# Down projection by seven block products over groups of feature tiles, in a hybrid decoder layer on one core

## The chip, the cores and the metric

The kernel runs on one core of a Trainium2 chip. The metric is the device time of one execution in microseconds (us); less is better.

## The reference

The layer normalises x (2048 tokens of width 1024, float32), runs two token mixers side by side, adds their output projection to the residual, and then does the part that this case is about:

```
hn = rms_norm(h, ffn_norm_w)
gate, up = split(hn @ w_gate_up)            # 1024 -> 2 x 2816
h = h + (silu(gate) * up) @ w_down          # 2816 -> 1024
return rms_norm(h, final_norm_w)
```

## The kernel before

The tokens are worked on in two halves of 1024; a half is two chunks (c) of 512 tokens, or eight tiles (g) of 128. The mixers of both halves come first, then for each half the up projection (`ffn_up`) and the down projection (`ffn_down`). One core has TensorE (PE), VectorE (DVE), ScalarE (ACT), GpSimd (POOL) and SyncE (SP), which issues all DMAs in order.

Every product of two float32 matrices is made of three matmuls: each operand is split into a high part, cast on ACT (L198), and the rest, a subtraction on DVE (L199). The high parts are multiplied with each other, and each with the other's rest. `split` is the helper; its source and its cast are both in SBUF.

The up projection already uses 2x2 blocks with seven products (p1 to p7) for a pair j of feature tiles (2 x 128 of the 2816 features, 11 pairs). Its results, four 128x512 tiles a11, a12, a21, a22 (feature tile, chunk), are written to DRAM by `store`. Element sums go through `tt_` (L484), on DVE or on GpSimd. The down projection takes the 22 feature tiles one by one for each chunk: it loads the activation tile (`ad`) and a 128x1024 weight tile (`raw_d`), splits both, and adds into eight PSUM banks (`pd`, L697 to L699), all of PSUM. After the last tile the banks are added to the residual `hd`, normalised (`rstd_of`: squares on ACT, a power on GpSimd) and scaled (L717).

`norm_h` belongs to the end of the mixers: for a token tile g it normalises h (`rstd_of`, squares `jk_hs` at L190; scaling at L816), transposes it on TensorE (`tp_hs`, L213), and ACT copies it out of PSUM (`hths`, L819). Five of these, for the second half, are left over and are called between the first seven products of the up projection of the first half. The framework orders the instructions of each engine by its own model; the written order is only a start.

Of the kernel before, what the change touches and what calls it, by code (L numbers as in the profile page):

```python
# [8 lines left out]
F32 = mybir.dt.float32  # L9
# [4 lines left out]
P = 128  # L14
# [8 lines left out]
T = 1024  # L23
# [12 lines left out]
def hybrid_layer(ctx: ExitStack, tc: tile.TileContext, x, x_t, norm_w, cols, w_in, gate_w, w_out, w_gu, w_down, out):  # L36
# [452 lines left out]

    def acts(src, nm):  # L490
        ops = {}
# [7 lines left out]
        def load(k):  # L499
            if k == 0:  # L500
                for name in ("p1", "p5", "p6", "p7", "p2"):
                    ops[name] = [block(f"act_{LET[name]}{s}_{nm}") for s in range(2)]
            b11, b12 = (xin(f"{t}{k}_{nm}") for t in ("b11_", "b12_"))
            b21, b22 = (page(f"{t}{k}_{nm}") for t in ("b21_", "b22_"))
# [10 lines left out]
        def two(k):  # L515
            b11, b12, b21, b22 = pages[k]
            tt_(b11, b22, b11, SUB_)
            tt_(b12, b22, b12, SUB_, nc.gpsimd)
            put("p2", k, b21)
            put("p6", k, b11)  # L520
            tt_(b21, b21, b11, SUB_)
            put("p7", k, b12)
            held.append((b22, b21))

# [10 lines left out]
        return ops, steps, [lambda: rest(0), lambda: rest(1)]  # L535

# [62 lines left out]
    def ffn_up(half, bops, between=()):  # L599
        between = list(between)  # L600
        q0 = half * 2 * NPAIR
        for q in range(q0, q0 + 2 * NPAIR):
# [7 lines left out]
            for i, name in enumerate(ORDER):  # L610
# [12 lines left out]
                elif name == "p7":  # L623
# [3 lines left out]
                    if m == 0:  # L627
                        nc.scalar.activation(out=e5, in_=e5, func=AF.Silu)
                        sg22 = e5
                    else:  # L630
                        tt_(e5, e5, sg22, MUL, nc.gpsimd)
                        store(half, j, 1, 1, e5)
                elif name == "p2":
                    if m == 0:
                        sg11 = page("sg11" + nm)
                        nc.scalar.activation(out=sg11, in_=b1, func=AF.Silu)
                    else:
                        tt_(sg11, sg11, b1, MUL)
                        store(half, j, 0, 0, sg11)
                elif name == "p3":  # L640
                    tt_(e1, u2, b3, ADD)
                    if m == 0:
                        nc.scalar.activation(out=e1, in_=e1, func=AF.Silu)
                        sg12 = e1
                    else:
                        tt_(e1, e1, sg12, MUL)
                        store(half, j, 0, 1, e1)
                else:
# [4 lines left out]
                    else:  # L653
                        tt_(u2, u2, sg21, MUL)
                        store(half, j, 1, 0, u2)
                if nxt is not None and not end:
# [7 lines left out]

    def store(half, j, u, c, p):
        nc.sync.dma_start(out=a_d[half][2 * j + u][c], in_=p)


    def ffn_down(half, c, extra=()):
        extra = list(extra)  # L670
# [3 lines left out]
        def ready(f):  # L674
            if f >= NF or f in ops:
                return
            nm = f"d{half}_{c}_{f}"
            p = xin("a" + nm)
# [6 lines left out]
            split((hi, lo), raw)  # L685
            ops[f] = (a, hi, lo)

        ready(0)
        for f in range(NF):
            ready(f + 1)  # L690
            ready(f + 2)
            a, whi, wlo = ops.pop(f)
            for tt in range(TPC):
                tsl = slice(tt * P, (tt + 1) * P)
                for n in range(2):
                    ps, nsl = banks[tt][n], slice(n * CW, (n + 1) * CW)
                    nc.tensor.matmul(ps, lhsT=a[:, 0, tsl], rhs=whi[:, nsl], start=(f == 0), stop=False)  # L697
                    nc.tensor.matmul(ps, lhsT=a[:, 0, tsl], rhs=wlo[:, nsl], start=False, stop=False)  # L698
                    nc.tensor.matmul(ps, lhsT=a[:, 1, tsl], rhs=whi[:, nsl], start=False, stop=(f == NF - 1))  # L699
            if f >= 6 and extra:  # L700
                extra.pop(0)()
        for e in extra:
            e()
        wfin = wvec(2, f"wfin{half}_{c}")
        for tt in range(TPC):
            g = c * TPC + tt
            r0 = half * T + g * P
            hp = []
            for n in range(2):
                p = page(f"hd{half}_{g}_{n}")  # L710
                nc.sync.dma_start(out=p, in_=h_d[half][g][n])
                tt_(p, p, banks[tt][n], ADD)
                hp.append(p)
            rs = rstd_of(hp, f"f{half}_{g}")
            for n in range(2):
                nsl = slice(n * CW, (n + 1) * CW)
                v.scalar_tensor_tensor(out=hp[n], in0=hp[n], scalar=rs, in1=wfin[:, nsl], op0=MUL, op1=MUL)  # L717
                nc.sync.dma_start(out=out[r0 : r0 + P, nsl], in_=hp[n])
# [3 lines left out]
    a_d = [[[dram.tile([P, CW], F32, name=f"a{i}_{k}_{c}") for c in range(2)] for k in range(NF)] for i in range(2)]  # L722

    bops = {}
    for half in range(2):
# [80 lines left out]
        else:  # L806
            bops[0], st, last = acts(hn_d[0], "0")
# [15 lines left out]

        later = []
        for c in range(NC):
            todo = len(steps[c])
            for n in range(2):
                wo = ws.take(4)
                for tt in range(TPC):
# [8 lines left out]
                    if n == 1:  # L838
                        later.append(lambda half=half, g=g, wffn=wffn, hp=hp: norm_h(half, g, wffn, hp))
                    while len(later) > 1 and (n, c) != (1, 1):  # L840
                        later.pop(0)()
                    i = n * TPC + tt + 1
                    while steps[c] and todo - len(steps[c]) < -(-todo * i // 8):
                        steps[c].pop(0)()
                    if half == 1 and c == 1 and n == 1 and tt == 0:
                        sums_start(0)
                        sums(0).make(0)
                        sums(0).done.add(0)
        if half == 0:
            xt = [b["xn"] for b in boxes]  # L850
# [11 lines left out]
    for half in range(2):  # L862
        ffn_up(half, bops[half], later if half == 0 else ())
        for c in range(NC):
            extra = ()
            if half == 0 and c == 1:
                bops[1], steps, last = acts(hn_d[1], "1")
                extra = steps + last
            ffn_down(half, c, extra)
        if half == 0:  # L870
            q = 2 * NPAIR
            sums_start(q)
# [3 lines left out]
            sums(q + 1).load(0)  # L876
            sums(q + 1).load(1)


# [66 lines left out]
```

## Time and profile before

| what | value |
|---|---|
| median of three runs | 2232.57 us (2226.35 to 2233.69) |
| profiled execution | 2235.64 us, of which its span is 2233.8 us |
| mean granted TensorE clock | 0.988 |
| TensorE busy | 2166.1 us, 97% of the span |
| down projection of the two halves | 1320 to 1559 us and 1984 to 2223 us of the span |

The span is what the profiler sees of the program; the 1.8 us beside it lie around it. A busy TensorE says that some matmul was under way, not how fast they follow each other.

### The profile page before, as it was taken

Reading aid. Unit: us, or ns where it says so; the run is one execution under the profiler, and the core shown is the slowest. Engines: PE = TensorE matmul, PEld = TensorE weight load, DVE = VectorE, ACT = ScalarE, POOL = GpSimd, SP = SyncE. Lnnn points to the kernel's source line nnn. Section 1 sums busy time; section 2 is a strip of 40 time slices with the busy share of each in tenths; the row PEclk is TensorE's granted clock in tenths of the full one; section 3 lists DMA queues with packets and bytes.
Section 4 is the critical chain, followed back from the end, with each engine's and each line's share of the span. In section 5 each row is a group of like instructions: output and inputs, shape, how many; then the busy total and the mean of one; then the engine's idle time right before and its main releaser. Section 6 shows DMA issues by size and latency. Waiting matters only on the chain.

```text
span 2233.8 us, 27050 instructions
## 1 busy us (share of the span) xinstructions
PE 2166.1 (97%) x10184; PEld 1787.4 (80%) x10184; DVE 1273.9 (57%) x2097; ACT 974.1 (44%) x1603; POOL 250.3 (11%) x229
## 2 busy tenths in 40 slices
PE   8999999999999999799999999999999999999998
PEld 6777788787777887688888888888788888888886
DVE  5577655635677458566565643584756565543534
ACT  5477754445667544433333332353333333322322
POOL 1111111101111001111111100010211011100000
PEclk9999999999999999899999999999999999999999
DMA  6111105741011166322222255573422222255552
GB/s 217 57 38 39 38 19 193 263 157 38 29 38 30 37 185 211 119 89 94 76 95 76 87 188 148 161 236 119 128 85 94 76 95 76 95 195 149 184 151 95
DMA packets 122899, 251.36 MB, mean 113 GB/s; under 512 B 11152, under 2 KB 27536, under 8 KB 122768
## 3 DMA queue, kind: packets, MB, share of 16 engines
q1 hardware_dynamic: 122768, 249.63, 35.3%
q8 instruction: 80, 1.31, 0.2%
q14 instruction: 51, 0.42, 0.1%
HBM read 201.35 MB, written 48.23 MB: 112 GB/s over the span
## 4 chain that ended last, share of the span: by engine, by line
PE 78%; ACT 9%; DVE 6%; DMA 3%; issue 1%; POOL 1%; SPq 0%; DVEq 0%; POOLq 0%; ACTq 0%
PE quad_g L579 11%; PE quad_e L579 11%; PE quad_a L579 11%; PE pd L699 7%; PE pd L698 7%; PE pd L697 7%; PE quad_f L579 5%; PE pb L226 1%; PE pb L227 1%; PE pb L225 1%; PE pa L225 1%; DMA raw_o<-in_w_out 1%; PE pa L226 1%; PE poh L238 1%; PE pa L227 1%
## 5 line engine op out<-in xcount | busy, mean ns | idle before, releaser
L698 PE MATMUL pd<-wlo_d,ad 128*128 128x512 f32 x704 | 273.9, 389 | 0.0
L697 PE MATMUL pd<-whi_d,ad 128*128 128x512 f32 x704 | 273.5, 389 | 0.0
L699 PE MATMUL pd<-whi_d,ad 128*128 128x512 f32 x704 | 273.2, 389 | 0.0
L199 DVE TENSOR_TENSOR ad<-ad,ad 128x512 fp32r<-128x512 f32 x88 | 62.4, 710 | 224.1 <-ACT ad L198 217.4
L198 ACT CAST ad<-ad 128x512 fp32r<-128x512 f32 x88 | 54.8, 623 | 289.2 <-PE pd L698 277.9
L484 POOL TENSOR_TENSOR e<-u,e 128x512 f32<-128x512 f32 x44 | 78.0, 1772 | 707.3 <-DVE u L484 367.8
L698 PEld LDWEIGHTS pd<-wlo_d,ad 128*128 128x128 f32 x704 | 132.1, 188 | 27.5
L697 PEld LDWEIGHTS pd<-whi_d,ad 128*128 128x128 f32 x704 | 132.2, 188 | 27.4
L699 PEld LDWEIGHTS pd<-whi_d,ad 128*128 128x128 f32 x704 | 132.2, 188 | 27.4
L579 PE MATMUL quad_f<-act_f,wgu_f 128*128 128x512 f32 x528 | 129.8, 395 | 4.8 <-DVE h L836 3.3
L579 PE MATMUL quad_e<-act_e,wgu_e 128*128 128x512 f32 x528 | 129.1, 393 | 2.8 <-ACT wgu_e L198 1.9
L579 PE MATMUL quad_a<-act_a,wgu_a 128*128 128x512 f32 x528 | 128.2, 392 | 0.0
L579 PE MATMUL quad_g<-act_g,wgu_g 128*128 128x512 f32 x528 | 127.4, 390 | 0.0
L579 PE MATMUL quad_g<-act_d,wgu_d 128*128 128x512 f32 x528 | 127.1, 389 | 0.0
L579 PE MATMUL quad_a<-act_b,wgu_b 128*128 128x512 f32 x528 | 127.0, 389 | 0.0
L579 PE MATMUL quad_e<-act_c,wgu_c 128*128 128x512 f32 x528 | 126.8, 389 | 0.0
L199 DVE TENSOR_TENSOR wlo_d<-raw_d,whi_d 128x1024 fp32r<-128x1024 f32 x88 | 110.0, 1250 | 22.6 <-ACT whi_d L198 18.4
L579 PEld LDWEIGHTS quad_f<-act_f,wgu_f 128*128 128x128 f32 x528 | 100.7, 191 | 26.5 <-ACT act_d L198 3.7
L579 PEld LDWEIGHTS quad_e<-act_e,wgu_e 128*128 128x128 f32 x528 | 100.0, 190 | 24.7 <-ACT wgu_e L198 2.4
L484 DVE TENSOR_TENSOR u<-u,quad_g 128x512 f32<-128x512 f32 x88 | 60.5, 687 | 100.0 <-PE quad_g L579 100.0
L579 PEld LDWEIGHTS quad_a<-act_a,wgu_a 128*128 128x128 f32 x528 | 99.9, 189 | 20.8
L579 PEld LDWEIGHTS quad_g<-act_g,wgu_g 128*128 128x128 f32 x528 | 99.5, 189 | 20.8
(260 smaller groups left out, 4698.5 us busy)
## 6 DMA issues: line engine op xcount, KB each, us to landing
raw<-in_w_gu SPq DMA_DIRECT2D x88, 512.0 KB, 4.1
raw_d<-in_w_down SPq DMA_DIRECT2D x88, 512.0 KB, 3.6
raw_in<-in_w_in SPq DMA_DIRECT2D x48, 512.0 KB, 3.6
ad<-a SPq DMA_DIRECT2D x88, 256.0 KB, 2.6
raw_o<-in_w_out SPq DMA_DIRECT2D x32, 512.0 KB, 4.5
a<-e SPq DMA_DIRECT2D x44, 256.0 KB, 4.2
x<-in_x SPq DMA_DIRECT2D x32, 256.0 KB, 5.4
xrh<-in_x SPq DMA_DIRECT2D x32, 256.0 KB, 4.0
```

The lines of the kernel that those rows point to most:

```text
L198: nc.scalar.copy(out=dst[0], in_=src)
L199: v.tensor_tensor(out=dst[1], in0=src, in1=f(dst[0]), op=ALU.subtract)
L225: nc.tensor.matmul(ps, lhsT=whi[:, ks], rhs=hi, start=(k == 0), stop=False)
L226: nc.tensor.matmul(ps, lhsT=wlo[:, ks], rhs=hi, start=False, stop=False)
L227: nc.tensor.matmul(ps, lhsT=whi[:, ks], rhs=lo, start=False, stop=(k == KT - 1))
L238: nc.tensor.matmul(ps, lhsT=hi, rhs=wlo[:, ks], start=False, stop=False)
L484: (e or v).tensor_tensor(out=out, in0=a, in1=b, op=op)
L579: nc.tensor.matmul(ps, lhsT=w[:, s, ks], rhs=x, start=first and k + n == 0, stop=k == 3 and n == 2, skip_group_check=not first)
L697: nc.tensor.matmul(ps, lhsT=a[:, 0, tsl], rhs=whi[:, nsl], start=(f == 0), stop=False)
L698: nc.tensor.matmul(ps, lhsT=a[:, 0, tsl], rhs=wlo[:, nsl], start=False, stop=False)
L699: nc.tensor.matmul(ps, lhsT=a[:, 1, tsl], rhs=whi[:, nsl], start=False, stop=(f == NF - 1))
```

## The change

The down projection becomes a 2x2 block product as well: feature tiles of a pair (u) and the two chunks on one side, feature tiles and the two column halves of the weights on the other. Seven products do the work of eight. A product runs over a group of four pairs (eight feature tiles), 48 matmuls of 128x512: four token tiles (tt), four pairs (q), three matmuls each. The first half has two such groups; its last three pairs are done as before (`down_plain`, 6 feature tiles). The second half has groups of four, four and three pairs.

The sums of activations are made on GpSimd in `store`, and seven tiles instead of four are written to DRAM. The sums of weights are made in place, on GpSimd (two of them in `make`, for p6, one for p1) and on DVE (`wdt`). The results are added to the residual in SBUF, which is now loaded before the first product: ACT copies p1 (`e1`) and p5 (`e5`) out of PSUM, DVE adds a bank to SBUF for five products, and GpSimd makes four additions per token tile. `norm_h` is cut into `scale_h` and `turn_h`, and a turn is called two places later than its scaling. In `acts` (operands of the second half's up projection) all seven pairs of blocks are now made at once. The diff, cut:

```diff
-    def store(half, j, u, c, p):
-        nc.sync.dma_start(out=a_d[half][2 * j + u][c], in_=p)
...
+    def store(half, j, a11, a12, a21, a22):
+        if (half, j) in PLAIN:
+            for u, c, p in ((0, 0, a11), (1, 0, a12), (0, 1, a21), (1, 1, a22)):
+                nc.sync.dma_start(out=a_d[half][2 * j + u][c], in_=p)
+            return
+        s1, s2, s3, s4 = (xin(f"as{i}_{half}_{j}") for i in range(4))
+        g = nc.gpsimd
+        tt_(s1, a21, a22, ADD, g)
+        tt_(s2, s1, a11, SUB_, g)
+        tt_(s3, a11, a21, SUB_, g)
+        tt_(s4, a12, s2, SUB_, g)
+        for name, p in (("p1", a11), ("p2", a12), ("p4", a22), ("p5", s1), ("p6", s2), ("p7", s3), ("p3", s4)):
+            nc.sync.dma_start(out=ao_d[half][name][j], in_=p)
...
+    DORDER = ("p1", "p2", "p6", "p5", "p3", "p7", "p4")
...
+        def make(self, i, q):
+            name = DORDER[i]
...
+            b = {k: t[:, q, :] for k, t in self.b.items()}
+            if name == "p6":
+                if q == 0:
+                    self.t2 = block(f"wdt_{self.nm}", F32)
+                tt_(self.t2[:, q, :], b[1, 1], b[0, 0], SUB_)
+            x = {"p1": b[0, 0], "p2": b[1, 0], "p5": b[0, 0], "p3": b[1, 1], "p7": b[0, 1], "p4": b[1, 0]}.get(name)
+            if name == "p6":
+                x = self.t2[:, q, :]
+            split([self.w[name][s][:, q, :] for s in range(2)], x)
+            split([self.a[name][q // 2][s][:, q % 2, :] for s in range(2)], self.raws[i][q // 2][:, q % 2, :])
+            if name == "p1":
+                tt_(b[0, 0], b[0, 1], b[0, 0], SUB_, nc.gpsimd)
+            elif name == "p6":
+                tt_(b[1, 0], b[1, 0], self.t2[:, q, :], SUB_, nc.gpsimd)
+                tt_(b[0, 1], b[1, 1], b[0, 1], SUB_, nc.gpsimd)
...
+        groups[0].load()
+        fetch(0)
+        for q in range(4):
+            make(0, q)
+        fetch(1)
+        for s, (gr, i) in enumerate(seq):
...
+            if name in ("p1", "p5"):
+                ma = [bank(f"pda{name[1]}_{tt}_{nm}") for tt in range(TPC)]
+            elif name in ("p6", "p7"):
+                mb = [aux(f"pdb{name[1]}_{tt}_{nm}") for tt in range(TPC)]
+            ps_ = mb if name in ("p6", "p7", "p4") else ma
+            a, w = gr.a.pop(name), gr.w.pop(name)
+            first = name in ("p1", "p6", "p5", "p7")
+            for tt in range(TPC):
...
+                for q in range(gr.n):
+                    ahi, alo = (a[q // 2][z][:, q % 2, tsl] for z in range(2))
+                    whi, wlo = (w[z][:, q, :] for z in range(2))
+                    for n, (x, y) in enumerate(((ahi, whi), (ahi, wlo), (alo, whi))):
+                        nc.tensor.matmul(
+                            ps, lhsT=x, rhs=y, start=first and q + n == 0, stop=q == gr.n - 1 and n == 2, skip_group_check=not first
+                        )
+                h00, h01 = hp[tt]
+                h10, h11 = hp[TPC + tt]
+                if name == "p1":
+                    e1[tt] = late(f"e1_{tt}_{nm}")
+                    nc.scalar.copy(out=e1[tt], in_=ps)
+                elif name == "p2":
+                    tt_(h00, h00, ps, ADD)
+                elif name == "p6":
+                    tt_(e1[tt], e1[tt], ps, ADD)
+                    tt_(h01, h01, e1[tt], ADD, nc.gpsimd)
+                elif name == "p5":
+                    e5[tt] = xin(f"e5_{tt}_{nm}")
+                    nc.scalar.copy(out=e5[tt], in_=ps)
+                    tt_(h10, h10, e1[tt], ADD, nc.gpsimd)
+                elif name == "p3":
+                    tt_(h01, h01, ps, ADD)
+                    tt_(h11, h11, e1[tt], ADD, nc.gpsimd)
+                    if end and last:
+                        finish(half, tt, hp[tt])
+                elif name == "p7":
+                    tt_(e5[tt], e5[tt], ps, ADD)
+                    tt_(h11, h11, e5[tt], ADD, nc.gpsimd)
+                else:
+                    tt_(h10, h10, ps, ADD)
+                    if end and last:
+                        finish(half, TPC + tt, hp[TPC + tt])
+                make(s + 1, tt)
...
+            if name == "p5" and not end:
+                groups[groups.index(gr) + 1].load()
...
-        def norm_h(half, g, wffn, hp):
-            nm = f"hs{half}_{g}"
-            rs = rstd_of(hp[g], nm)
+        def scale_h(half, g, wffn, hp):
+            rs = rstd_of(hp[g], f"hs{half}_{g}")
             for n in range(2):
                 p = hp[g][n]
                 v.scalar_tensor_tensor(out=p, in0=p, scalar=rs, in1=wffn[:, n * CW : (n + 1) * CW], op0=MUL, op1=MUL)
-                pt = transposed(g, n, p, nm)
+
+        def turn_h(half, g, hp):
+            nm = f"hs{half}_{g}"
+            for n in range(2):
+                pt = transposed(g, n, hp[g][n], nm)
...
-        later = []
+        later, turns = [], []
...
                     if n == 1:
-                        later.append(lambda half=half, g=g, wffn=wffn, hp=hp: norm_h(half, g, wffn, hp))
-                    while len(later) > 1 and (n, c) != (1, 1):
-                        later.pop(0)()
+                        later.append(lambda half=half, g=g, wffn=wffn, hp=hp: scale_h(half, g, wffn, hp))
+                        turns.append(lambda half=half, g=g, hp=hp: turn_h(half, g, hp))
+                    if (n, c) != (1, 1):
+                        if len(turns) > 2 or (n == 0 and turns):
+                            turns.pop(0)()
+                        if later:
+                            later.pop(0)()
...
+        later = [lambda a=later, b=turns, i=i: ([a.pop(0)()] if a else 0, b.pop(0)() if i > 1 and b else 0) for i in range(7)]
...
     for half in range(2):
         ffn_up(half, bops[half], later if half == 0 else ())
-        for c in range(NC):
...
-            ffn_down(half, c, extra)
+        hp = residual(half)
         if half == 0:
+            down_quads(0, ((0, 4), (4, 4)), hp, False)
+            bops[1], steps, last = acts(hn_d[1], "1", True)
+            extra = steps + last
+            for c in range(NC):
+                down_plain(0, c, range(16, NF), hp, extra)
...
+        else:
+            down_quads(1, ((0, 4), (4, 4), (8, 3)), hp, True)
```

Three places show how the instructions move. The first is ACT in the first products of the up projection. Before, the squares of token tile 5, 6 or 7 (`jk_hs1_5`) stand behind the copy of the transposed tile ahead of it (`hths1_4`):

```order
L819 COPY hths1_4_0_7405<-tp_hs1_4_0_7400 128x512
L819 COPY hths1_4_1_7414<-tp_hs1_4_1_7409 128x512
L190 ACTIVATE jk_hs1_5_0_7437,ss_hs1_5_7436<-h1_5_0_6994 128x512
L198 CAST wgu_f_0_0_1_7433<-s20_0_1_7431 128x512
L190 ACTIVATE jk_hs1_5_1_7439,ss_hs1_5_7436<-h1_5_1_7189 128x512
L651 ACTIVATE u20_0_0_7429<-u20_0_0_7429 128x512
L819 COPY hths1_5_0_7449<-tp_hs1_5_0_7444 128x512
L819 COPY hths1_5_1_7458<-tp_hs1_5_1_7453 128x512
L190 ACTIVATE jk_hs1_6_0_7483,ss_hs1_6_7482<-h1_6_0_7033 128x512
L198 CAST wgu_g_0_0_1_7479<-s30_0_1_7477 128x512
L198 CAST wgu_b_0_0_1_7521<-raw1_0_0_1_7323 128x512
L190 ACTIVATE jk_hs1_6_1_7485,ss_hs1_6_7482<-h1_6_1_7228 128x512
```

After the change:

```order
L190 ACTIVATE jk_hs1_5_0_7340,ss_hs1_5_7339<-h1_5_0_6941 128x512
L190 ACTIVATE jk_hs1_5_1_7342,ss_hs1_5_7339<-h1_5_1_7152 128x512
L198 CAST wgu_e_0_0_1_7336<-s10_0_1_7334 128x512
L190 ACTIVATE jk_hs1_6_0_7368,ss_hs1_6_7367<-h1_6_0_6996 128x512
L190 ACTIVATE jk_hs1_6_1_7370,ss_hs1_6_7367<-h1_6_1_7191 128x512
L973 COPY hths1_4_0_7381<-tp_hs1_4_0_7376 128x512
L198 CAST wgu_f_0_0_1_7364<-s20_0_1_7362 128x512
L973 COPY hths1_4_1_7389<-tp_hs1_4_1_7384 128x512
L190 ACTIVATE jk_hs1_7_0_7414,ss_hs1_7_7413<-h1_7_0_7039 128x512
L631 ACTIVATE e50_0_0_7332<-e50_0_0_7332 128x512
L639 ACTIVATE sg110_0_0_7450<-quad_a_0_0_0_7288 128x512
L190 ACTIVATE jk_hs1_7_1_7416,ss_hs1_7_7413<-h1_7_1_7226 128x512
```

The squares of tiles 5, 6 and 7 now stand ahead of the copies of tile 5.

The second place is DVE inside the down projection of the second half. Before, it holds splits alone (`ad` activations, `wlo_d` weights):

```order
L199 TENSOR_TENSOR ad1_0_11_15668<-ad1_0_11_15666,ad1_0_11_15668 128x512
L199 TENSOR_TENSOR wlo_d1_0_11_15674<-raw_d1_0_11_15671,whi_d1_0_11_15673 128x1024
L199 TENSOR_TENSOR ad1_0_12_15703<-ad1_0_12_15701,ad1_0_12_15703 128x512
L199 TENSOR_TENSOR wlo_d1_0_12_15709<-raw_d1_0_12_15706,whi_d1_0_12_15708 128x1024
L199 TENSOR_TENSOR ad1_0_13_15738<-ad1_0_13_15736,ad1_0_13_15738 128x512
L199 TENSOR_TENSOR wlo_d1_0_13_15744<-raw_d1_0_13_15741,whi_d1_0_13_15743 128x1024
```

After, at the end of the second group's p7: additions from PSUM into the residual (`hd`) and `e5`, the splits of the operands of p4 (`aop_d`), and the weight sum of the third group (`wdt`):

```order
L484 TENSOR_TENSOR hd1_2_1_15575<-hd1_2_1_15575,pda5_2_1_4_16520 128x512
L199 TENSOR_TENSOR aop_d10_1_4_16719<-ra_d0_1_4_16656,aop_d00_1_4_16718 128x512 x2
L199 TENSOR_TENSOR aop_d12_1_4_16761<-ra_d2_1_4_16658,aop_d02_1_4_16760 128x512
L484 TENSOR_TENSOR wdt_1_8_16945<-wdby_1_8_16614,wdax_1_8_16608 128x512
L199 TENSOR_TENSOR aop_d12_1_4_16761<-ra_d2_1_4_16658,aop_d02_1_4_16760 128x512
L484 TENSOR_TENSOR wdt_1_8_16945<-wdby_1_8_16614,wdax_1_8_16608 128x512
L484 TENSOR_TENSOR hd1_3_1_15577<-hd1_3_1_15577,pda5_3_1_4_16521 128x512
L484 TENSOR_TENSOR wdt_1_8_16945<-wdby_1_8_16614,wdax_1_8_16608 128x512
L484 TENSOR_TENSOR e5_0_1_4_16534<-e5_0_1_4_16534,pdb7_0_1_4_16698 128x512
L484 TENSOR_TENSOR e5_1_1_4_16557<-e5_1_1_4_16557,pdb7_1_1_4_16699 128x512
L484 TENSOR_TENSOR e5_2_1_4_16580<-e5_2_1_4_16580,pdb7_2_1_4_16700 128x512
```

The evictions `e5` of p7, into whose banks p4 accumulates, stand behind the splits for p4 and three weight sums.

The third place is ACT at the entry of the first half's down projection. Before, casts of activations and weights tile by tile, and the up projection's copies among them:

```order
L198 CAST ad0_0_0_10470<-ad0_0_0_10468 128x512
L643 ACTIVATE e10_10_0_10236<-e10_10_0_10236 128x512
L198 CAST whi_d0_0_0_10475<-raw_d0_0_0_10473 128x1024
L651 ACTIVATE u20_10_0_10272<-u20_10_0_10272 128x512
L616 COPY e10_10_1_10369<-quad_a_0_10_1_10353 128x512
L619 COPY e50_10_1_10383<-quad_e_0_10_1_10354 128x512
L198 CAST ad0_0_1_10481<-ad0_0_1_10479 128x512
L198 CAST whi_d0_0_1_10486<-raw_d0_0_1_10484 128x1024
```

After, with the casts for p6 (`wd_f`), p5 (`wd_e`) and p3 (`wd_c`):

```order
L198 CAST wd_f0_0_0_10659<-wdt_0_0_10663 128x512
L198 CAST aop_f00_0_0_10661<-ra_f0_0_0_10604 128x512 x2
L198 CAST wd_e0_0_0_10755<-wdax_0_0_10518 128x512 x4
L198 CAST wd_f0_0_0_10659<-wdt_0_0_10663 128x512 x2
L198 CAST wd_c0_0_0_10842<-wdby_0_0_10524 128x512 x4
L841 COPY e1_0_0_0_10576<-pda1_0_0_0_10560 128x512
L198 CAST wd_f0_0_0_10659<-wdt_0_0_10663 128x512
L841 COPY e1_1_0_0_10598<-pda1_1_0_0_10561 128x512
L841 COPY e1_2_0_0_10620<-pda1_2_0_0_10562 128x512
```

The copies `e1` of p1, into whose banks p2 accumulates, stand behind casts of weights for later products.

## Rows read from the trace of the kernel before

**Rows 1.** The page, part 1: busy time of each engine, share, instructions.

```profile
PE 2166.1 (97%) x10184; PEld 1787.4 (80%) x10184; DVE 1273.9 (57%) x2097; ACT 974.1 (44%) x1603; POOL 250.3 (11%) x229
```

**Rows 2.** Windows: stretch, length, busy time and count by engine, granted clock, DMA.

```profile
1300.00:1350.00 50.00, 50.00 (x222) 41.43 (x221) 20.72 (x23) 13.87 (x18) 3.45 (x2) 1.00 0.68 223
...
2000.00:2050.00 50.00, 50.00 (x222) 41.38 (x222) 17.40 (x19) 14.94 (x20) 0.00 (x0) 1.00 0.51 147
```

**Rows 3.** The same for the tiles pd alone (TensorE, weight loads, VectorE).

```profile
1984.00:2104.00 120.00, 120.00 (x530) 99.38 (x530) 3.51 (x6) 1.00 0.56 168
```

**Rows 4.** TensorE's waits, 870 to 925: total us, times, longest.

```profile
PE tp_hs L213 <- DVE h L816: 11.3, 3, 4.7
```

**Rows 5.** The chain that ended last, in order of time, 905 to 912.

```profile
905.07 1.95 PE tp_hs L213 x8
...
907.04 0.58 ACT hths L819
907.63 0.62 ACT jk_hs L190 x2
...
910.81 0.76 DVE h L816
```

**Rows 6.** Timeline of TensorE, transposes: start, length; in brackets idle time, releaser.

```profile
899.45 1.03 PE L213 MATMUL tp_hs<-ident,h 128*128 128x128 f32 x8
...
905.07 1.94 PE L213 MATMUL tp_hs<-ident,h 128*128 128x128 f32 x8 [2.96 <-DVE h L816]
```

**Rows 7.** Windows around the same place.

```profile
905.00:910.00 5.00, 1.94 (x8) 1.57 (x8) 2.40 (x5) 3.44 (x8) 0.00 (x0) 0.50 0.44 119
```

**Rows 8.** Groups by line: busy us, mean ns, idle before, releaser.

```profile
L698 PE MATMUL pd<-wlo_d,ad 128*128 128x512 f32 x704 | 273.9, 389 | 0.0
...
L199 DVE TENSOR_TENSOR ad<-ad,ad 128x512 fp32r<-128x512 f32 x88 | 62.4, 710 | 224.1 <-ACT ad L198 217.4 <-DMA raw_d<-in_w_down 6.5
...
L199 DVE TENSOR_TENSOR wlo_d<-raw_d,whi_d 128x1024 fp32r<-128x1024 f32 x88 | 110.0, 1250 | 22.6 <-ACT whi_d L198 18.4 <-PE quad_a L579 4.2
...
L484 DVE TENSOR_TENSOR hd<-hd,pd 128x512 f32<-128x512 f32 x32 | 20.8, 684 | 14.0 <-PE pd L699 14.0
...
L717 DVE SCALAR_TENSOR_TENSOR hd<-hd,ss_f,wfin 128x512 f32<-128x512 f32 x32 | 22.3, 747 | 1.9 <-POOL ss_f L193 1.9
...
L198 ACT CAST ad<-ad 128x512 fp32r<-128x512 f32 x88 | 54.8, 623 | 289.2 <-PE pd L698 277.9 <-PE quad_a L579 8.8 <-PE quad_e L579 2.5
...
L484 POOL TENSOR_TENSOR e<-u,e 128x512 f32<-128x512 f32 x44 | 78.0, 1772 | 707.3 <-DVE u L484 367.8 <-ACT wgu_c L198 291.7 <-issue 34.7
...
L484 POOL TENSOR_TENSOR e<-e,e 128x512 f32<-128x512 f32 x22 | 28.9, 1312 | 1.7
```

**Rows 9.** Timeline of VectorE, two instructions back to back.

```profile
951.42 0.68 DVE L199 TENSOR_TENSOR wgu_b<-raw,wgu_b 128x512 fp32r<-128x512 f32 x1
952.02 0.68 DVE L484 TENSOR_TENSOR u<-u,quad_g 128x512 f32<-128x512 f32 x1
```

**Rows 10.** Timeline of VectorE and GpSimd, 1046 to 1050.

```profile
1046.14 0.69 DVE L199 TENSOR_TENSOR wgu_c<-s,wgu_c 128x512 fp32r<-128x512 f32 x1
1048.15 0.69 DVE L484 TENSOR_TENSOR sg<-sg,quad_a 128x512 f32<-128x512 f32 x1 [1.32 <-PE quad_a L579]
1048.86 1.05 DVE L199 TENSOR_TENSOR wgu_d<-raw,wgu_d 128x512 fp32r<-128x512 f32 x1
...
1046.31 1.67 POOL L484 TENSOR_TENSOR e<-u,e 128x512 f32<-128x512 f32 x1 [17.37 <-ACT wgu_c L198]
1048.06 1.30 POOL L484 TENSOR_TENSOR e<-e,e 128x512 f32<-128x512 f32 x1
```

**Rows 11.** DMA issues: count, KB each, median us to landing.

```profile
raw_d<-in_w_down SPq DMA_DIRECT2D x88, 512.0 KB, 3.6
```

**Rows 12.** Timeline: the last matmul, and the last work of VectorE.

```profile
2223.09 0.39 PE L699 MATMUL pd<-whi_d,ad 128*128 128x512 f32 x1
...
2228.95 1.42 DVE L717 SCALAR_TENSOR_TENSOR hd<-hd,ss_f,wfin 128x512 f32<-128x512 f32 x2 [0.73 <-POOL ss_f L193]
```

More of the change, by code (lines that the diff above doesn't have):

```diff
@@ L500, in load @@
             if k == 0:
-                for name in ("p1", "p5", "p6", "p7", "p2"):
+                for name in ("p1", "p5", "p6", "p7", "p2") + (("p3", "p4") if direct else ()):
                     ops[name] = [block(f"act_{LET[name]}{s}_{nm}") for s in range(2)]
             b11, b12 = (xin(f"{t}{k}_{nm}") for t in ("b11_", "b12_"))
-            b21, b22 = (page(f"{t}{k}_{nm}") for t in ("b21_", "b22_"))
+            b21, b22 = ((late if direct else page)(f"{t}{k}_{nm}") for t in ("b21_", "b22_"))
             for p, n, c in ((b11, 0, 0), (b12, 0, 1), (b22, 1, 1), (b21, 1, 0)):
@@ L522, in two @@
             put("p7", k, b12)
+            if direct:
+                put("p3", k, b22)
+                put("p4", k, b21)
             held.append((b22, b21))
@@ L534, in acts @@
             steps.append(lambda k=k: two(k))
-        return ops, steps, [lambda: rest(0), lambda: rest(1)]
+        return ops, steps, [] if direct else [lambda: rest(0), lambda: rest(1)]
     ORDER = ("p1", "p5", "p6", "p7", "p2", "p3", "p4")
@@ L631, in ffn_up @@
                         tt_(e5, e5, sg22, MUL, nc.gpsimd)
-                        store(half, j, 1, 1, e5)
+                        a22 = e5
                 elif name == "p2":
@@ L638, in ffn_up @@
                         tt_(sg11, sg11, b1, MUL)
-                        store(half, j, 0, 0, sg11)
+                        a11 = sg11
                 elif name == "p3":
@@ L646, in ffn_up @@
                         tt_(e1, e1, sg12, MUL)
-                        store(half, j, 0, 1, e1)
+                        a21 = e1
                 else:
@@ L654, in ffn_up @@
                         tt_(u2, u2, sg21, MUL)
-                        store(half, j, 1, 0, u2)
+                        store(half, j, a11, u2, a21, a22)
                 if nxt is not None and not end:
@@ L685, in ready @@
             split((hi, lo), raw)
-            ops[f] = (a, hi, lo)
+            ops[i] = (a, hi, lo)
         ready(0)
[L689 to L692, printed above, removed]
+        for i in range(len(fs)):
+            ready(i + 1)
+            ready(i + 2)
+            a, whi, wlo = ops.pop(i)
             for tt in range(TPC):
@@ L701, in ffn_down @@
+            if extra:
                 extra.pop(0)()
-        for e in extra:
-            e()
-        wfin = wvec(2, f"wfin{half}_{c}")
         for tt in range(TPC):
             g = c * TPC + tt
-            r0 = half * T + g * P
-            hp = []
             for n in range(2):
[L710 to L718, printed above, removed]
+                tt_(hp[g][n], hp[g][n], banks[tt][n], ADD)
@@ new lines, in down_plain, with finish @@
+            finish(half, g, hp[g])
+    def finish(half, g, hp):
+        if g not in fin:
+            fin[g] = wvec(2, f"wfin{half}_{g}") if g % TPC == 0 else fin[g - 1]
+        r0 = half * T + g * P
+        rs = rstd_of(hp, f"f{half}_{g}")
+        for n in range(2):
+            nsl = slice(n * CW, (n + 1) * CW)
+            v.scalar_tensor_tensor(out=hp[n], in0=hp[n], scalar=rs, in1=fin[g][:, nsl], op0=MUL, op1=MUL)
+            nc.sync.dma_start(out=out[r0 : r0 + P, nsl], in_=hp[n])
+    fin = {}
@@ L724, in hybrid_layer @@
+    ao_d = [{name: dram.tile([NPAIR, P, CW], F32, name=f"ao{i}_{name}") for name in ORDER} for i in range(2)]
     bops = {}
@@ L863, in hybrid_layer @@
         ffn_up(half, bops[half], later if half == 0 else ())
-        for c in range(NC):
[L865 to L868, printed above, removed]
-            ffn_down(half, c, extra)
-        if half == 0:
+        hp = residual(half)
+        if half == 0:
+            down_quads(0, ((0, 4), (4, 4)), hp, False)
[3 more added lines that the diff above has]
+                down_plain(0, c, range(16, NF), hp, extra)
+            fin.clear()
             q = 2 * NPAIR
```

71 lines of the change are left out of this document (61 added, 10 removed).

## The prediction

> **What bounds the kernel now.** I began with the page's busy times: TensorE is busy 97% of the span and nothing else is above 57% [rows 1]. So a change is worth what it takes off TensorE, less what TensorE must newly wait for. The windows come next. The entry into the first half's down projection and the middle of the second's have no gap, and in the latter VectorE works 17.4 us of 50, ScalarE 14.9 and GpSimd not at all [rows 2]. There is room beside TensorE there, and the question is whether the new work fits into it.
>
> The price of a matmul must not be taken from the groups by line: they give 389 ns for a 128x512 matmul [rows 8], but matmuls overlap. 530 of them pass in 120 us [rows 3], one per 226 ns, and this pace is what a removed matmul gives back.
>
> TensorE's waits show one place that the second part of the change touches: 11.3 us in three waits of the transposes for scaled tiles [rows 4]. The chain shows the loop behind them: eight transposes, a copy by ScalarE, the squares of the next token tile, which stand behind that copy on ScalarE, a power, the scaling by VectorE, the next eight transposes [rows 5]. The granted clock is at 0.50 there, so 1.2 of 2.4 GHz [rows 7], after those waits had begun; eight transposes take 1.94 us instead of 1.03 [rows 6].
>
> **The change part by part.**
>
> *Matmuls.* Before, a half has 2 chunks x 22 tiles x 24 = 1056 in the down projection. A group of four pairs takes 7 x 48 = 336 where it took 384. The first half becomes 2 x 336 + 2 x 6 x 24 = 960, the second 336 + 336 + 252 = 924. That is 228 fewer; times 226 ns, **-51.6 us**. The weight loads go with their matmuls.
>
> *Transposes.* TensorE still has them almost where they were, but ScalarE now has the squares of tiles 5, 6 and 7 ahead of the copies, so the loop is cut: the scalings can follow each other. To be had are 11.3 us of waiting and 3 x (1.94 - 1.03) = 2.7 us at the lower clock, 14.0 in all. VectorE must still evict p3 before it scales tile 7, so I leave a little: **-13** (bounds -14 and -5, the latter if two of three waits stay).
>
> *VectorE and GpSimd in a group of four pairs.* A group lasts 336 x 226 ns = 76 us on TensorE. VectorE gets 56 splits, 4 weight sums and 20 evictions, GpSimd 12 weight sums and 16 additions; ScalarE 56 casts at 623 ns [rows 8] and 8 copies, 40 us, which fits. VectorE's instructions take 0.69 us each, but back to back they start 0.60 apart [rows 9], so 48 us. GpSimd's addition takes 1.30 us when it meets nothing [rows 10], so 36 us. Each fits alone.
>
> They do not run side by side, though. A subtraction of VectorE begun at 1046.14 ended at 1046.83; GpSimd's addition, begun at 1046.31 beside it, ended 1.15 us after that. At 1048.86 VectorE's split took 1.05 us and ended 0.55 after GpSimd's addition [rows 10]. An eviction from PSUM (1048.15) kept its 0.69 beside a GpSimd addition. So instructions of VectorE with two SBUF operands and GpSimd's take turns, at 0.55 and 1.15 us a turn, and evictions are free of it. The means agree: GpSimd's 1772 ns against 1312 [rows 8]. Over a group the turns sum to 60 x 0.55 + 28 x 1.15 = 65 us, with evictions in line 77, against 76: no loss on average, but no slack either where the work bunches.
>
> It bunches where another group follows. Between the first eviction of p6 and the start of p4 there are p6's remaining three quarters, p5, p3 and p7: 40.7 us. Into these fall 20 of GpSimd's 28 instructions (three additions per token tile with e1, and eight sums for the next group), 26 of VectorE's two-operand instructions and 8 evictions: 20 x 1.15 + 26 x 0.55 + 8 x 0.60 = 42.1 us, and part of it can't begin before TensorE has finished p6. What is late at the end is the row that the order shows: e5 behind the splits for p4 and the weight sums. TensorE's p4 needs both, the banks and the operands. I take 2.5 us for each of the three groups that another follows, and 2.5 more for the clock, which fell in the trace after such waits: **+10**. Bounds: nothing, if evictions hide GpSimd's turns; 9 us a group if each holds the other for its whole length (20 x 1.30 + 34 x 0.69 = 49.5).
>
> The Trainium skill (SBUF — State Buffer, "Who interferes with whom") speaks against this change: a VectorE instruction with two SBUF inputs and a GpSimd instruction that reads SBUF need the same port pair, whoever begins first has it for the whole instruction, and the other blocks fully. The trace agrees on who blocks and on the PSUM exception, but the hand-over overlaps by 0.15 us on either side. By the page's words the sum would be that of the third rival below.
>
> *Last group.* Three pairs last 57 us, and normalising moves in: 16 scalings of 0.75 us [rows 8] and eight powers, the latter behind GpSimd's additions. VectorE's splits for p4 stand behind scalings that wait for a power. **+4** (0 to 12).
>
> *Entries.* The weights of the first group need buffers that the last up-projection products free from 16 us before its end on (six products of 12 x 226 ns). 4.2 MB at the 223 GB/s that the window at 1300 shows [rows 2] take 19 us and land 3 us after the end; at one 512 KB load per 3.6 us [rows 11] they would take 29. p1 and p2 need only the first two blocks. But ScalarE has casts for p5 and p3, which need the last block and four GpSimd sums, ahead of the copies e1, and p2 adds into those banks 10.9 us after p1 begins. 3 + 5 + 10 casts x 0.62 is past that by some 2 to 3 us: **+4** for two entries (0 to 16).
>
> *Rest of the first half.* 288 matmuls, 65 us. VectorE has 12 activation and weight splits (0.71 + 1.25), 36 instructions for the second half's operands, 16 evictions and 16 scalings: 64 us by lengths. It just fits; before, this had twice the time. **+3** (0 to 10).
>
> *Covered.* The four GpSimd sums of `store` (1.3 us each per pair, 5 of 38 us) precede the next addition that ScalarE waits for by three products; if that cover went, ScalarE would wait 5 us a pair. DMA: a group moves 11.5 MB in 76 us, 151 GB/s, below the 168 of now [rows 3]. The tail from the last matmul, 2223.09, to the last scaling at 2228.95 and the last store has the same steps [rows 12]: 0 (-3 to +4).
>
> Sum: -51.6 - 13 + 10 + 4 + 4 + 3 = **-43.6**. Against the profiled 2235.6 us (span 2233.8 and 1.8 around it) this gives 2192. That execution stood 3 us above the median, so I forecast **2189 us**. All terms at their best give 2235.6 - 51.6 - 14 - 3 - 3 = 2164; all at their worst 2235.6 - 51.6 - 5 + 27 + 12 + 16 + 10 + 4 - 3 = 2245.
>
> **The rivals.**
>
> *All of it hidden.* Evictions and VectorE's idle time take in GpSimd's turns, and weights split ahead carry TensorE over: 2164 to 2178. For it: VectorE's sum per group is 65 us of 76 by turns. Against: the bunching before p4.
>
> *Waits about twice as long, or transposes still late.* TensorE's order keeps the turns within the last products of the first quad, as before; were the scalings late again, 13 us return: 2202. Waits of 4 us rather than 2.5 at every group and entry end there too: 2200 to 2224. For it: PE's order; against: ScalarE's.
>
> *VectorE and GpSimd become the bound (slower).* Each instruction holds the other for its whole length, and evictions, which wait for TensorE in the same queue, hide nothing. A group of four then needs 60 x 0.69 + 28 x 1.30 + 20 x 0.69 = 91.6 us, 15.5 over TensorE; the group of three 45 x 0.69 + 25 x 1.30 + 13.8 = 77.4, 20 over. 4 x 15.5 + 20 + 11 of the other terms take 93 of the 64.6 gained: 2232.6 + 28 = 2261. It decides from 64.6 us over 35 products, 1.85 us a product. For it: GpSimd's worst instructions; against: both hand-overs above, and evictions untouched by GpSimd.
>
> **How the numbers follow.** The forecast case (2178 to 2200) gets 0.5, all hidden 0.17, longer waits 0.2, the bound 0.13, of which about half would end within 0.3% of 2232.6 (2226 to 2239). About 0.3% is what a measurement of this kernel can tell from no change. So faster 0.87, same 0.06, slower 0.07. The range leaves out the bound, and the ends of the first and third case: 2168 to 2224.
>
> **What would show it.** Right: about 1884 down-projection matmuls at 226 ns; tp_hs with no waits above 2 us; TensorE's waits in the products at p4's first bank, released by VectorE (e5 or the split aop_d), in the three groups that another follows; two-operand VectorE instructions of 1.0 to 1.8 us in those stretches; waits for e1 copies at the first p2 of each half. Wrong: waits in every product, GpSimd busy without a break (the bound), or TensorE's clock at 0.50 through long stretches of the products.

## The result, and the profile after

| kernel | median, us | range | ratio to before, 95% |
|---|---|---|---|
| before | 2233.13 (4 runs) | 2226.35 to 2233.95 | |
| changed | 2209.57 (4 runs) | 2208.05 to 2211.54 | 0.9902 [0.9881, 0.9923] |

Faster by 23.6 us, about half of the 43.6 that the prediction summed. The page's busy times after the change, which answer to [rows 1]:

```profile
PE 2121.9 (96%) x9956; PEld 1744.7 (79%) x9956; DVE 1508.5 (68%) x2314; ACT 1019.4 (46%) x1757; POOL 587.7 (27%) x442
```

The 228 matmuls are gone (10184 to 9956), but TensorE is busy only 44.2 us less, and it waits more. GpSimd's busy time has more than doubled.

TensorE's waits around the transposes, 868 to 925 us (columns as in [rows 4]):

```profile
PE tp_hs L213 <- ACT hths L973: 2.0, 1, 2.0
PE tp_hs L213 <- DVE h L966: 1.9, 2, 1.5
```

There were 11.3 us. The last of these transposes now end at 898 us, and the granted clock, 0.50 at them before [rows 7], is at full over the stretch that holds most of them (same columns as in [rows 2]):

```profile
880.00:900.00 20.00, 17.58 (x88) 13.72 (x87) 18.49 (x31) 13.04 (x31) 5.13 (x4) 1.00 0.41 131
```

One more wait of the kernel before, which [rows 4] does not show, is gone as well. A product of the up projection waited behind an addition of the mixers to h (L836), and its twelve matmuls took 5.46 us, at a granted clock of 0.50; after the change the same twelve take 2.89 us without a wait. The line is from the timeline of the kernel before:

```profile
884.48 5.46 PE L579 MATMUL quad_f<-act_f,wgu_f 128*128 128x512 f32 x12 [3.30 <-DVE h L836]
```

TensorE's waits in the down projection, first half (1290 to 1545 us), then second half (1955 to 2210):

```profile
PE pda L834 <- DVE aop_c L199: 8.1, 2, 7.4
PE pd L721 <- ACT act_d L198: 3.6, 1, 3.6
PE pdb L834 <- DVE wd_f L199: 3.2, 1, 3.2
...
PE pda L834 <- DVE aop_c L199: 7.6, 2, 7.4
PE pdb L834 <- DVE wd_f L199: 3.0, 1, 3.0
PE pda L834 <- ACT aop_e L198: 1.2, 1, 1.2
PE pdb L834 <- ACT wd_f L198: 1.0, 1, 1.0
PE pdb L834 <- DVE e L484: 0.7, 1, 0.7
```

`aop_c` is the activation operand of p3, `wd_f` the weight operand of p6, `e` the additions that free p4's banks. Within the groups, the large waits lie in the first group of each half; 3.6 us stand in the plain part, at the change of chunk. The forecast place, p4, has 1.7 us, all in the second group of the second half: the 0.7 behind `e`, and the 1.0 put down to `wd_f`, a cast for a later product that p4 does not read. An addition `e` ended just before p4's matmuls began:

```profile
2127.07 8.44 PE L834 MATMUL pdb<-wd_d,aop_d 128*128 128x512 f32 x36 [1.01 <-ACT wd_f L198]
...
2126.25 1.87 DVE L484 TENSOR_TENSOR e<-e,pdb 128x512 f32<-128x512 f32 x3
```

Four windows show the rest: in each half, the stretch from the entry to the end of p3 in the first group, then the stretch behind it.

```profile
1290.00:1371.00 81.00, 69.66 (x284) 55.65 (x283) 76.72 (x77) 34.90 (x66) 55.19 (x34) 0.92 0.60 210
1371.00:1449.00 78.00, 78.00 (x346) 64.59 (x345) 56.66 (x76) 29.66 (x54) 30.61 (x20) 1.00 0.39 119
1958.00:2039.00 81.00, 67.79 (x273) 53.00 (x272) 77.75 (x71) 32.56 (x62) 61.94 (x38) 0.92 0.60 215
2039.00:2115.00 76.00, 76.00 (x337) 62.92 (x336) 65.78 (x75) 33.17 (x60) 40.07 (x25) 1.00 0.39 128
```

In the second row of each half TensorE has no gap, at one matmul per 226 ns. In the first row of each VectorE is busy 95 or 96% (76.72 and 77.75 of 81), with about as many instructions as in the second, and GpSimd has 34 and 38 instructions instead of 20 and 25. The timeline of VectorE, GpSimd and TensorE at the longest wait:

```profile
1346.08 2.37 DVE L199 TENSOR_TENSOR aop_c<-ra_c,aop_c 128x512 fp32r<-128x512 f32 x2
1348.37 6.79 DVE L199 TENSOR_TENSOR wd_a<-wdax,wd_a 128x512 fp32r<-128x512 f32 x4
1355.09 3.43 DVE L199 TENSOR_TENSOR aop_c<-ra_c,aop_c 128x512 fp32r<-128x512 f32 x2
...
1346.24 5.03 POOL L484 TENSOR_TENSOR hd<-hd,e 128x512 f32<-128x512 f32 x3 [1.83 <-DVE e L484]
1351.23 6.74 POOL L484 TENSOR_TENSOR wdax<-wday,wdax 128x512 f32<-128x512 f32 x4
...
1348.51 0.97 PE L834 MATMUL pda<-wd_c,aop_c 128*128 128x512 f32 x3 [0.73 <-DVE aop_c L199]
1356.89 7.32 PE L834 MATMUL pda<-wd_c,aop_c 128*128 128x512 f32 x17 [7.42 <-DVE aop_c L199]
```

Four splits of the next group's weights (`wd_a`), which TensorE wants much later, stand ahead of the last splits of p3's activations, and they start 1.68 us apart, in turn with GpSimd. The 17 matmuls behind the wait take 0.43 us each: the clock fell to 1.2 GHz after it.

```profile
1353.00:1363.00 10.00, 6.08 (x13) 4.35 (x14) 10.00 (x7) 3.52 (x8) 10.00 (x7) 0.50 0.19 56
```

Not all of VectorE's time before this went into turns. It also stood idle for ScalarE's cast of p5's activations, and ScalarE for their load (in the second half too, 3.25 us):

```profile
1336.79 3.06 DVE L199 TENSOR_TENSOR aop_e<-ra_e,aop_e 128x512 fp32r<-128x512 f32 x2 [3.20 <-ACT aop_e L198]
...
1336.13 1.14 ACT L198 CAST aop_e<-ra_e 128x512 fp32r<-128x512 f32 x2 [3.29 <-DMA ra_e<-ao_p]
```

How much of the wait at p3 goes back to that load in this kernel, no run separates.

In all, the first half took 242 us for 960 matmuls and the second 231 for 924; at 226 ns they are 217 and 209. 47 us were lost, where the prediction had 21. By place, from one product's first matmul to the next one's, and rounded: p3 of the two first groups 12 and 11 (48 matmuls in 23.0 and 21.7 us instead of 10.9); the entries up to p6 5 and 6; p5 of the second half 2; the plain part 8; p7 and p4 of the second half's second group 2; the last group nothing. The tail is as before [rows 12]: the last scaling ended 6.3 us after the last matmul, where it was 6.9.

### The profile page after: what moved, and what is told of

It is laid out like the page before. It is cut to its first block, busy times and chain, and to the rows that moved or that the text cites. A ratio compares the mean times of both kernels' runs of the same rounds, so it can differ in the third digit from the quotient of the medians.

```text
span 2206.3 us, 27183 instructions
## 1 busy us (share of the span) xinstructions
PE 2121.9 (96%) x9956; PEld 1744.7 (79%) x9956; DVE 1508.5 (68%) x2314; ACT 1019.4 (46%) x1757; POOL 587.7 (27%) x442
## 5 line engine op out<-in xcount | busy, mean ns | idle before, releaser
L484 POOL TENSOR_TENSOR hd<-hd,e 128x512 f32<-128x512 f32 x80 | 121.5, 1550 | 142.4 <-DVE e L484 142.3
L582 PEld LDWEIGHTS quad_a<-act_b,wgu_b 128*128 128x128 f32 x528 | 99.1, 188 | 20.6
L582 PEld LDWEIGHTS quad_e<-act_c,wgu_c 128*128 128x128 f32 x528 | 99.1, 188 | 20.6
L582 PEld LDWEIGHTS quad_g<-act_d,wgu_d 128*128 128x128 f32 x528 | 98.9, 188 | 20.4
L226 PE MATMUL pb<-xn,wlo_in 128*128 128x512 f32 x256 | 102.7, 401 | 0.0
L225 PE MATMUL pb<-xn,whi_in 128*128 128x512 f32 x256 | 102.4, 400 | 0.0
L227 PE MATMUL pb<-xn,whi_in 128*128 128x512 f32 x256 | 101.8, 398 | 0.0
L155 DVE TENSOR_TENSOR wlo_in<-raw_in,whi_in 128x1024 fp32r<-128x1024 f32 x48 | 60.7, 1265 | 60.0 <-PE pv L238 40.6
L226 PE MATMUL pa<-xn,wlo_in 128*128 128x512 f32 x256 | 100.9, 394 | 0.0
```

What stands on the lines that cost most here:

```text
L155: v.tensor_tensor(out=lo, in0=raw, in1=f(hi), op=ALU.subtract)
L225: nc.tensor.matmul(ps, lhsT=whi[:, ks], rhs=hi, start=(k == 0), stop=False)
L226: nc.tensor.matmul(ps, lhsT=wlo[:, ks], rhs=hi, start=False, stop=False)
L227: nc.tensor.matmul(ps, lhsT=whi[:, ks], rhs=lo, start=False, stop=(k == KT - 1))
L484: (e or v).tensor_tensor(out=out, in0=a, in1=b, op=op)
L582: nc.tensor.matmul(ps, lhsT=w[:, s, ks], rhs=x, start=first and k + n == 0, stop=k == 3 and n == 2, skip_group_check=not first)
```

## The experiments

All ratios are to the kernel before, run beside each kernel; its median there was 2230 to 2233 us.

**The transposes alone.** The kernel before with `scale_h` and `turn_h`, and nothing else of the change.

> The kernel before with one part of the change alone: norm_h cut into scale_h and turn_h, turns called later; the down projection stays with eight products. The stages of the two traces say that TensorE reached the first down product 21.9 us earlier after the change (3.6 in the mixers, 18.3 between the first seven-product group and the down projection). Theory A: all of that belongs to the moved transposes, so this kernel takes 2233 - 22 = 2211 us (2207 to 2215), and the seven products themselves gave only about 2 us. Rival, the term of the prediction: the transposes give 13 us, 2220 (2218 to 2224), and the rest of the earlier start comes from the other edits (store, acts, buffers).

2211.15 us, 0.9913 [0.99, 0.9927]: 19.4 us at 2230. The waits for `tp_hs` are 3.8 us, as in the changed kernel. Theory A holds; the term was larger than 13. The wait of `quad_f` for h is gone here too, and it is back (3.3 us) in the next run, which undoes this part.

**The products alone.** The changed kernel with `norm_h` whole again.

> The changed kernel with its second part undone: norm_h whole again and called where it was before, the seven products as in the change. The moved transposes alone gave 18.6 us (e1_turns), the whole change about 22 against the same runs. Theory A (the two parts add): the seven products alone give only 2 to 5 us, so this kernel takes 2226 us where before takes 2230 (2222 to 2230), although it has 228 matmuls fewer, 51.6 us. Rival I (the parts help or hinder each other: with the late transposes the operands of the first product are ready earlier than TensorE wants them, or the reverse): 2218 us or less, or 2233 or more.

2226.10 us, 0.9978 [0.9969, 0.9986]: 4.9 us. The two parts add within the intervals (19.4 + 4.9 against 21.8). So seven products instead of eight, 51.6 us of matmuls, were worth about 5 us as they stood.

**Order alone.** The changed kernel, with VectorE's early splits behind p3's (diff cut; `z` is the last split of a product's activations):

```diff
-            split([self.w[name][s][:, q, :] for s in range(2)], x)
+            with tc.issue_after(gate[0]) if name == "p4" or (name == "p1" and gate[0] is not None) else nullcontext():
+                split([self.w[name][s][:, q, :] for s in range(2)], x)
+            z = split([self.a[name][q // 2][s][:, q % 2, :] for s in range(2)], self.raws[i][q // 2][:, q % 2, :])
+            if name == "p3":
+                gate[0] = z.ins
```

> The changed kernel with one dependence of order added on VectorE: the splits of p4's weights (wd_d) and of the next group's p1 weights (wd_a) are issued behind the last split of p3's activations (aop_c); same instructions, only these eight stand later in each half's first group. Theory A (a wrong place in VectorE's queue, made long by the turns with GpSimd): the two waits of 7.6 us at p3 shrink to under 1.5, the 10.2 us at half clock behind each go too (5 us each), so 2209.6 - 22 = about 2187 us (2182 to 2194). Rival B (VectorE and GpSimd together are simply behind by then, whatever the order): the waits reappear at p7, p4 or the next p1, and the time stays within 2203 to 2212.

2207.46 us, 0.9898 [0.9885, 0.9912], the same as the changed kernel. The wait at p3 is gone, but TensorE's waits (total, times, longest) are now these:

```profile
PE pdb L839 <- ACT wd_f L198: 12.4, 3, 6.4
PE pdb L839 <- DVE wd_f L199: 6.2, 2, 3.2
PE pdb L839 <- DVE aop_g L199: 4.2, 5, 1.3
```

12.0 of the 12.4 us are two waits at p4. TensorE's and VectorE's timeline at one of them:

```profile
1374.16 3.32 PE L839 MATMUL pdb<-wd_d,aop_d 128*128 128x512 f32 x7 [5.60 <-ACT wd_f L198]
...
1370.58 2.83 DVE L484 TENSOR_TENSOR wdt<-wdby,wdax 128x512 f32<-128x512 f32 x2
1373.33 1.87 DVE L484 TENSOR_TENSOR e<-e,pdb 128x512 f32<-128x512 f32 x3
```

The releaser named there is a cast for a later product; p4 does not read it. What p4's first bank needs is the addition of 1373.33 (0.67 us), and that stood behind the next group's `wdt`. My theory, that this one place in the queue was the cause, falls: the time is the rival's, VectorE and GpSimd together were behind, and the order chose where it showed. Here it showed at p4, the place of the prediction, and the down projection lost 45 us in all, where it had lost 47. One other order was tried; that none would do better is not shown.

**The sums on VectorE.** The changed kernel with `, nc.gpsimd` struck from the seven `tt_` calls in `make` and `down_quads`.

> The changed kernel with the 28 GpSimd sums of a group of the down projection (12 of weights, 16 of results) done by VectorE instead; GpSimd keeps the sums of activations in store. Theory A (a pair of turns costs 1.70 us, and VectorE back to back needs 0.60 for each of the two): VectorE gets 108 instructions a group, 65 us of 76, its instructions return to 0.68, and the waits at p6 and p3 go: 2175 to 2195 us. Rival C (VectorE becomes the bound, since its queue has less slack than the turns left it): waits in most products, 2210 us or more.

2167.83 us, 0.9724 [0.971, 0.9737]: 40 us better than the change, below the low end of what I expected. The page's busy times and the first half's two stretches:

```profile
PE 2109.9 (97%) x9956; PEld 1741.6 (80%) x9956; DVE 1489.0 (69%) x2451; ACT 1019.4 (47%) x1757; POOL 374.6 (17%) x305
...
1290.00:1371.00 81.00, 81.00 (x359) 67.11 (x358) 81.00 (x132) 40.67 (x76) 3.25 (x2) 1.00 0.63 224
1371.00:1449.00 78.00, 78.00 (x345) 64.61 (x345) 57.38 (x91) 28.93 (x52) 1.30 (x1) 1.00 0.43 132
```

VectorE took 137 instructions more and was busy 19.5 us less. In the first stretch it does 132 instead of 77, without a pause, and TensorE does not wait. The same `wd_a`, without turns (compare 1348.37 above):

```profile
1338.06 1.28 DVE L199 TENSOR_TENSOR aop_c<-ra_c,aop_c 128x512 fp32r<-128x512 f32 x2
1339.27 2.49 DVE L199 TENSOR_TENSOR wd_a<-wdax,wd_a 128x512 fp32r<-128x512 f32 x4
```

**The sums left out.**

> The changed kernel without the 28 GpSimd sums of a group of the down projection: the sums of weights for p1, p6 and the four additions per token tile are left out, so the output is another one; the order on VectorE stays, wd_a and wd_d still ahead of the last aop_c. It is the time with no turns in the down groups. Theory A: VectorE's splits take 0.68, nothing is late at p6 and p3, both halves of the down projection come near their matmuls (217 and 209 us) plus 3 to 8 us: 2165 to 2182 us. Rival D (the losses come from the order, the loads and the entries, not from GpSimd): the waits at p3 and p6 remain at over half their size, 2192 us or more.

2166.83 us, 0.9716 [0.9703, 0.973]. With nothing to do for these sums the kernel is no faster than with them on VectorE, so they cost nothing there that can be measured. VectorE's order, with `wd_a` still ahead of the last `aop_c`, does no harm without GpSimd's sums: TensorE does not wait at p3.

```profile
1332.18 2.49 DVE L199 TENSOR_TENSOR wd_a<-wdax,wd_a 128x512 fp32r<-128x512 f32 x4
1334.59 1.28 DVE L199 TENSOR_TENSOR aop_c<-ra_c,aop_c 128x512 fp32r<-128x512 f32 x2
```

**GpSimd busy for nobody.** Is it the turns, or results of GpSimd that someone waited for? The kernel of the last run, with 28 additions a group into a tile that is not used:

```diff
+    spare = sc_t[0].rearrange("p a b -> p (a b)")
+
+    def idle(p):
+        tt_(spare, spare, p, ADD, nc.gpsimd)
...
+            if name == "p1":
+                idle(b[0, 1])
+            elif name == "p6":
+                idle(b[1, 0])
+                idle(b[0, 1])
```

> e4_none (GpSimd's 28 sums left out, so another output; 2167 us) with 28 additions of the same size put back on GpSimd at the same places, each reading the tile that the left-out sum read, and writing a tile that nobody uses. VectorE's queue is that of e4_none. Theory A (turns: GpSimd's instructions lengthen VectorE's, whoever waits for their results): most of the 40 us come back, 2190 to 2212, VectorE's splits at 1.7 us beside them. Rival H (the loss came from results of GpSimd that VectorE, ScalarE or TensorE waited for): the time stays at 2165 to 2176.

2195.94 us, 0.9851 [0.9836, 0.9865]: 30 of the 41 us come back, though nobody needs these results. TensorE's waits in the products (total, times, longest) are released by VectorE and ScalarE, none by GpSimd:

```profile
PE pda L839 <- ACT e L846: 7.9, 3, 5.6
PE pdb L839 <- DVE aop_f L199: 5.4, 1, 5.4
...
PE pda L839 <- DVE aop_e L199: 3.1, 1, 3.1
PE pda L839 <- DVE aop_b L199: 3.0, 2, 2.2
```

So turns without any result to wait for cost a time of this size; that is shown. But none of these waits is at p3, so it is not shown that three quarters of the change's own loss are turns. About 3 of the 30 us lie in the plain part, where loads also waited for tiles that the unused additions read. The other 11 us fit waits for GpSimd's results and a different order of waits; no run separates these.

**One kind of sum at a time.** The weight sums on VectorE, additions on GpSimd:

> The changed kernel with the 12 sums of weights of a group on VectorE and the 16 additions of results still on GpSimd. With none on GpSimd (e3_dve) the time was 2168, with all 28 2208. Theory A (each turn costs alike, wherever it falls): 2168 + 40 x 16/28 = 2191 us (2183 to 2199). Rival F (one kind alone carries the loss: the additions, which bunch at p5 and p3): 2200 us or more here, and e6_adve near 2170; or the sums of weights do, and this kernel is at 2172 or less.

2184.47 us, 0.9795 [0.9778, 0.9811]. The additions on VectorE, weight sums on GpSimd:

> The changed kernel with the 16 additions of results of a group on VectorE and the 12 sums of weights still on GpSimd. Theory A: 2168 + 40 x 12/28 = 2185 us (2177 to 2193), with the waits at p6 of each half's first group (3.2 us each) still there. Rival F: near 2170 if the additions carried the whole loss, 2200 or more if the sums of weights did.

2189.08 us, 0.9815 [0.98, 0.9829]. Neither kind carries the loss alone, and both times lie in the ranges of theory A. Against the change, moving the 12 weight sums of a group gives 24 us and moving the 16 additions 19, both 40; so turns do not all cost alike. In the first of the two kernels the waits at p6 are gone and those at p3 stay (10.9 us for `aop_c`); in the second those at p6 stay (6.2 for `wd_f`), p3's go, and 5.2 us appear at p4.

**The plain pairs.** The sums on VectorE, and:

```diff
-            if extra:
+            if extra and (c or i < 5):
                 extra.pop(0)()
```

This edit holds back one step: five stand in the first chunk instead of six. The expectation speaks of three, and its times were worked out for that.

> e3_dve with one edit in the plain last pairs of the first half: the steps that make the second half's operands are called at every second tile of the first chunk, so that three instead of six stand there. In e3_dve TensorE waits 5.5 us at the change of chunk (1481.7 us), where the activation tile was loaded too late because its buffers were held by those steps, and 6.8 us at half clock follow. Theory A: both go, 2168 - 5.5 - 3.4 = 2159 us (2156 to 2163). Rival G: VectorE's work there only just fits, so five steps in the second chunk make its end or the first product of the next half late: 2164 to 2172.

2165.20 us, 0.9705 [0.9691, 0.972]. TensorE's waits in the plain part:

```profile
PE pd L721 <- DVE hd L484: 1.5, 1, 1.5
...
PE pd L722 <- DVE wlo_d L199: 1.1, 1, 1.1
```

They were 3.9 and 0.3 (not the 5.5 of the expectation), with a granted clock of 0.53 behind them, which is now 1.00. The plain part took 72.7 us from its first matmul to its last, and takes 68.4. The kernel is 2.6 us better by the medians; the intervals overlap, so by time alone it is not settled. Neither theory was tested, since three steps were not tried. This is the best kernel of the study, 65.8 us below before at 2230.

## Why the prediction was half right

- **Matmuls, -51.6**: right in count, and right in pace wherever nothing waits (266 in 60 us).
- **Transposes, -13**: the mechanism was right, the size is 18 to 19. I counted only the three waits of [rows 4] and three lengthened groups of transposes. The wait of `quad_f` for h (3.3 us) went with them, and so did the lower clock in the matmuls beside them: the twelve of `quad_f` and, from 918.86, twelve more that took 4.12 us instead of 2.88. Why the wait for h goes when the transposes move was not looked into.
- **Three groups followed by another, +10**: the step that failed; about 28 were lost. The price of a turn was right (0.55 and 1.15 make 1.70; `wd_a` starts 1.68 apart). The load was not: I gave every group its own 60 and 28 instructions in 76 us and found only p4 short. But the first group of a half starts with no lead. Its own twelve weight sums, its additions, eight sums and several splits of the next group, which the framework pulls forward, and the last sums of the up projection fall into one stretch: 34 to 38 GpSimd instructions. At 34 turns of 1.15, 62 two-operand VectorE instructions of 0.55 and 15 others of 0.60 that is 82 us, an estimate, in a stretch of 81 in which part of the work cannot begin before a product ends. The two first groups lost 23 us at p3, clock included, and 2 at p5; at their p4 they lost nothing. The forecast wait at p4 came in one group of the three, and 2 us were lost there. That the missing lead is what makes the first group short is read from these counts; the runs show that its waits go with GpSimd's sums.
- **Entries, +4**: about 11. Not the copies e1 behind casts, which cost 0.3 us in the second half, but p6's operand `wd_f`, 3.2 and 3.0 us behind twelve weight sums in turn with VectorE, and a lower clock after each. In the run with the unused additions it was the copies, by 5.6 us.
- **Rest of the first half, +3**: about 8 with the clock. The activation tile of the second chunk came late, and VectorE's addition that frees the first bank ended 0.5 us later still; both stand behind steps for the second half, and 4 us go when one step is moved. The lengths that the prediction names for VectorE here add up to 71 us, not 64, so by its own figures the work did not fit into 65.
- **Last group, +4**: nothing. **Tail, 0**: right.

The sum with what was measured is -51.6 - 19 + 28 + 11 + 8 + 0 = -23.6, where -23.6 was measured. That it meets to the decimal is rounding: the result and the run with the transposes alone are each known to 3 to 5 us. The time lies in the band of the second rival (2200 to 2224): waits were longer than forecast, as it says, but in the first groups and not in every group, and the transposes were not late. Of the signs named in advance, the pace of the matmuls, the transposes' waits and the VectorE instructions of 1.7 us came; the waits at p4 in three groups and for e1 did not. What would show it wrong did not occur either: no waits in every product, no bound by VectorE and GpSimd in all groups (the third rival, 2261), half clock for some 10 us behind each long wait, not through long stretches.

By the Trainium skill (SBUF — State Buffer, "Who interferes with whom") issue order decides who blocks, for whole instructions. The alternation at 1.70 us, against 0.69 + 1.30 for whole lengths, is a little better than that; the blocking itself is as the Trainium skill says. The Trainium skill (GPSIMD Engine Reference, "4.1 Engine selection") would put elementwise sums on VectorE. The run with the sums there agrees, by 40 us.

## What to carry to other kernels

Before giving GpSimd work to relieve VectorE, price the pair: here a turn of both took 1.70 us, while VectorE alone does both instructions in 1.20, so the offload took more of VectorE than it gave. Sum such a load over the stretch where it bunches (the first group after an entry, with what the scheduler pulls forward), not over the average group. When a reordering only moves a wait, ask whether the engine behind it is short of time rather than of order; here it was, since the waits went with GpSimd's sums and not with the order.

## What had not been expected of the hardware

VectorE and GpSimd do not always take turns. In the run with the unused additions one of GpSimd's stood for 5.82 us while VectorE issued two-operand splits back to back at full pace; only after VectorE paused did they alternate.

```profile
1341.67 2.49 DVE L199 TENSOR_TENSOR wd_a<-wdax,wd_a 128x512 fp32r<-128x512 f32 x4
1344.08 1.28 DVE L199 TENSOR_TENSOR aop_c<-ra_c,aop_c 128x512 fp32r<-128x512 f32 x2
1346.06 6.12 DVE L199 TENSOR_TENSOR aop_g<-ra_g,aop_g 128x512 fp32r<-128x512 f32 x4 [0.70 <-ACT e L854]
...
1340.69 5.82 POOL L484 TENSOR_TENSOR sct<-sct,e 128x512 f32<-128x512 f32 x1 [4.58 <-DVE e L484]
```

With the weight sums on GpSimd alone one of them stood for 10.05 us. What makes a sequence alternate and not hold out was not settled.
